# The opening of a two-layer decoder trunk: every block of tokens turned once, unscaled, and scaled behind the turn

## The chip, the cores and the metric

The kernel runs on one core of one Trainium2 chip. The metric is the device time of one execution in microseconds; the time given for a kernel is the median of its runs. In the profile TensorE is PE (its weight loads PEld), VectorE is DVE, ScalarE is ACT, GpSimd is POOL, and SP is the queue that issues nearly all DMAs.

## The reference

x is a stream of 1024 tokens of 1024 features in float32. There are two layers; each normalises x, makes all projections from it in one matrix, mixes tokens in two ways, and then runs a gated feed-forward part. Only the beginning of the first layer matters here:

```
def rmsnorm(x, g):
    xf = x.astype(jnp.float32)
    y = xf * lax.rsqrt(jnp.mean(xf * xf, axis=-1, keepdims=True) + RMS_EPS)
    return (y * g.astype(jnp.float32)).astype(x.dtype)
...
for l in range(DEPTH):
    h = rmsnorm(x, norm1[l])
    proj = h @ w_in[l]
    qa, ka, va, qb, kb, vb, gate_pre = jnp.split(proj, splits, axis=-1)
    ...
    x = x + merged @ w_o[l]
    h2 = rmsnorm(x, norm2[l])
    ...
return rmsnorm(x, norm_f)
```

## The kernel before, in words

**Numbers in two parts.** A float32 product is made from three TensorE passes: each operand is a rounded part `hi` and the rest `lo`, and `product` (lines 182 to 184) issues hi x hi, hi x lo and lo x hi. `split` (lines 141 and 148) makes the parts: ACT casts to `hi`, DVE subtracts to `lo`. For h the parts are `hh` and `hl`. TensorE wants features on the partitions, so h is held turned: `H[n]` holds the parts for token half n (512 tokens), with eight feature blocks `k` of 128. Beside it, `RAW[n, k]` holds the turned h unsplit (`h_raw`); its only readers are sums of blocks, made by DVE behind the last block's `hl`.

**The opening** is the generator `first()`. It brings in x in eight blocks of 128 tokens (`xr`, four buffers; the load of a block waits until the block four before it is released). For each block ACT squares and sums (line 2006) and takes the root (line 2007), DVE takes the reciprocal (line 2008): the factor of each token, in `factor[i]`. Then there are two forms.

- Blocks 0, 1 and 2: DVE multiplies the block in token order by the factor and the gain in two instructions of 128x512 (line 2015); the gain for that is spread over all partitions once, by eight transposes into the banks `gb` (line 2078). The scaled block `xsq` is turned by eight transposes (line 1997, `x_t`), and `in_two` splits it straight out of the bank. As the residual needs x turned and unscaled, `xr` is turned too, by eight more transposes, and copied by ACT to `x_part` (line 2024, `kept`); pairs of blocks are stored to DRAM as `xs` (line 2026).
- Blocks 3 to 7: the block is turned once, unscaled, and copied to `x_part`. One transpose spreads the factor over the partitions (line 2036, `x_rb`). DVE multiplies `x_part` by gain and factor, eight instructions of 128x128 (line 2040), into `RAW`; `split` makes the parts from there.

`RAW[0]` is missing blocks 0 to 2 that way; `again` (line 2055) lets GpSimd add `hh` and `hl` for these 384 tokens, in two groups of four additions, when blocks 4 and 5 are handled. A memset of `slots` on GpSimd is ordered behind them.

The weights of the first product (`w_raw`, four pairs of feature blocks) are cast by ACT (`weights_hi`) and their rest is subtracted by DVE for pairs 0 and 2, by GpSimd for pairs 4 and 6 (`weights_lo`, line 1990).

**What sets the order.** TensorE runs in the order of the text in the whole kernel. `mixer` alternates one step of `first()` with units of the first product (`v_ps`, twelve matmuls each, four feature blocks of one token block; later `kq_ps` and `q_ps`): setup and block 0, a unit; block 1's transposes, a unit; block 2's transposes, two units; block 3's, two units, and so on. A unit uses the block one or two behind the one just turned. ACT and DVE run in the order of the text up to block 2 (though a planner may slip other instructions in between); from block 3 on the planner orders them by readiness and priority, and `tc.high_priority` lifts an instruction. `fill(n)` is n matmuls of the identity whose result is not used; each is two passes in the profile.

## Time and profile before

| | |
|---|---|
| median of 3 runs | 2615.91 us (2615.09 to 2616.14) |
| profiled execution | 2618.04 us, its span 2616.1 us |
| TensorE busy in the span | 2606.0 us |
| DVE busy | 2089.5 us |
| ACT busy | 1357.6 us |
| GpSimd busy | 102.2 us |

A row of the timeline gives start and duration in us, the engine, the line, the operation, output<-inputs, shapes and count; in brackets stands the time that the engine had idled before it, and what ended that. Several instructions in a row are merged with their total. Starts count from the beginning of the span. The windows give for each stretch the busy time of each engine and its number of instructions.

### The profile page before, as it was taken

The numbers are of one execution on the slowest core, as the hardware profiler recorded it, in microseconds if no ns is written. First come the engines' busy times: TensorE is split into PE (matmuls) and PEld (weight loads), VectorE is DVE, ScalarE is ACT, GpSimd is POOL, SyncE is SP. The second block draws the span as 40 slices with busy tenths as digits, with TensorE's granted clock in tenths as the row PEclk, the third lists the DMA queues.
The fourth block names the chain that finished last, engine by engine and source line by source line (L and its number), as shares of the span: only waits on it lengthen the run. The fifth ranks groups of instructions, "written<-read, shape, count | busy, mean of one in ns | idle before, by whom it ended". The sixth has DMA issues, their size and how long they took to land.

```text
span 2616.1 us, 36210 instructions
## 1 busy us (share of the span) xinstructions
PE 2606.0 (100%) x12736; PEld 2185.2 (84%) x12736; DVE 2089.5 (80%) x3484; ACT 1357.6 (52%) x2533; POOL 102.2 (4%) x135
## 2 busy tenths in 40 slices
PE   9999999999999999999999999999999999999999
PEld 8888888888888888888888888888888888888888
DVE  7877777795988888897677788777869888889965
ACT  6555666574554555422445555666645555544225
POOL 3000000020000000000000000000300000000000
PEclk9999999999999999999999999999999999999999
DMA  7434578873344444688344436787633344447962
GB/s 254 151 120 132 161 207 217 214 247 93 93 145 153 145 164 142 234 326 317 145 145 147 125 128 180 203 231 210 207 99 119 125 161 146 150 164 260 347 238 111
DMA packets 400418, 468.22 MB, mean 179 GB/s; under 512 B 24308, under 2 KB 315500, under 8 KB 398444
## 3 DMA queue, kind: packets, MB, share of 16 engines
q1 hardware_dynamic: 400220, 465.90, 55.3%
q8 instruction: 101, 1.65, 0.3%
q14 instruction: 81, 0.66, 0.1%
q10 hardware_dynamic: 16, 0.00, 0.0%
HBM read 303.23 MB, written 162.59 MB: 178 GB/s over the span
## 4 chain that ended last, share of the span: by engine, by line
PE 96%; DVE 1%; DMA 1%; ACT 1%; issue 1%; SPq 0%; POOL 0%; DVEq 0%; ACTq 0%
PE u_a L1019 6%; PE u_a L1018 6%; PE u_a L1017 6%; PE d_ps L1780 5%; PE d_ps L1781 5%; PE d_ps L1782 5%; PE i_a L1017 5%; PE i_a L1019 5%; PE i_a L1018 5%; PE u_c L1017 3%; PE u_c L1019 3%; PE u_c L1018 3%; PE i_c L1017 3%; PE i_c L1019 3%; PE i_c L1018 3%; PE o_ps L183 2%
## 5 line engine op out<-in xcount | busy, mean ns | idle before, releaser
L141 ACT CAST w_hi<-up_a 128x512 fp32r<-128x512 f32 x280 | 173.9, 622 | 276.5 <-DVE up_a L1634 120.5
L148 DVE TENSOR_TENSOR w_lo<-up_a,w_hi 128x512 fp32r<-128x512 f32 x280 | 189.3, 688 | 83.6 <-ACT w_hi L141 83.6
L141 ACT CAST w_hi<-in_a 128x512 fp32r<-128x512 f32 x252 | 156.2, 622 | 162.9 <-PE i_c L1018 38.0
L148 DVE TENSOR_TENSOR w_lo<-in_a,w_hi 128x512 fp32r<-128x512 f32 x252 | 172.7, 687 | 75.8 <-ACT w_hi L141 67.0
L1788 DVE TENSOR_TENSOR x<-x,d_ps 128x512 f32<-128x512 f32 (+1 forms) x228 | 153.4, 674 | 65.0 <-PE d_ps L1782 61.6
L1780 PE MATMUL d_ps<-gd_in,w_hi 128*128 128x512 f32 (+1 forms) x340 | 130.0, 382 | 0.0
L1782 PE MATMUL d_ps<-gd_in,w_lo 128*128 128x512 f32 (+1 forms) x340 | 129.8, 382 | 0.0
L1781 PE MATMUL d_ps<-gd_in,w_hi 128*128 128x512 f32 (+1 forms) x340 | 129.7, 382 | 0.0
L1019 PE MATMUL u_a<-hh,w_lo 128*128 128x512 f32 x320 | 124.5, 389 | 0.0
L1018 PE MATMUL u_a<-hl,w_hi 128*128 128x512 f32 x320 | 124.5, 389 | 0.0
L1017 PE MATMUL u_a<-hh,w_hi 128*128 128x512 f32 x320 | 124.5, 389 | 0.0
L1017 PE MATMUL u_a<-t_hi,w_hi 128*128 128x512 f32 x320 | 124.5, 389 | 0.0
L1019 PE MATMUL u_a<-t_hi,w_lo 128*128 128x512 f32 x320 | 124.5, 389 | 0.0
L1018 PE MATMUL u_a<-t_lo,w_hi 128*128 128x512 f32 x320 | 124.5, 389 | 0.0
L1017 PE MATMUL i_a<-hh,w_hi 128*128 128x512 f32 x288 | 119.2, 414 | 0.0
L1017 PE MATMUL i_a<-t_hi,w_hi 128*128 128x512 f32 x288 | 118.3, 411 | 0.0
L1780 PE MATMUL d_ps<-gd_in,wd 128*128 128x512 f32 (+1 forms) x292 | 113.9, 390 | 0.0
L1019 PE MATMUL i_a<-hh,w_lo 128*128 128x512 f32 x288 | 113.2, 393 | 0.0
L1019 PE MATMUL i_a<-t_hi,w_lo 128*128 128x512 f32 x288 | 113.0, 393 | 0.0
L1018 PE MATMUL i_a<-t_lo,w_hi 128*128 128x512 f32 x288 | 112.9, 392 | 0.0
L1018 PE MATMUL i_a<-hl,w_hi 128*128 128x512 f32 x288 | 112.8, 392 | 0.0
L1782 PE MATMUL d_ps<-gd_in,wd 128*128 128x512 f32 (+1 forms) x292 | 112.8, 386 | 0.0
(380 smaller groups left out, 7834.9 us busy)
## 6 DMA issues: line engine op xcount, KB each, us to landing
gd<-g SPq DMA_DIRECT2D x154, 512.0 KB, 3.3
gd_in<-gd SPq DMA_DIRECT2D x154, 512.0 KB, 5.9
up_a<-in_w_up_dram SPq DMA_DIRECT2D x80, 512.0 KB, 5.2
in_a<-in_w_in_dram SPq DMA_DIRECT2D x72, 512.0 KB, 5.3
wd_raw<-in_w_down_dram SPq DMA_DIRECT2D x22, 1024.0 KB, 11.2
gin<-gs SPq DMA_DIRECT2D x32, 512.0 KB, 3.8
w_raw<-in_w_o_dram SPq DMA_DIRECT2D x64, 256.0 KB, 2.9
gs<-u SPq DMA_DIRECT2D x48, 256.0 KB, 3.2
```

What stands on the lines that cost most here:

```text
L141: one = act.copy(hi, src)
L148: two = dve.tensor_tensor(lo, src, f32(hi), ALU.subtract)
L183: pe.matmul(o, lh, rl, start=False, stop=False, skip_group_check=share)
L1017: pe.matmul(o, w[0][:, c], rh, start=(first and i == 0), stop=False, skip_group_check=True)
L1018: pe.matmul(o, w[0][:, c], rl, start=False, stop=False, skip_group_check=True)
L1019: pe.matmul(o, w[1][:, c], rh, start=False, stop=(last and i == 3), skip_group_check=True)
L1780: pe.matmul(o[:, sub], wh[:, c], gh[:, sub], start=(i == 0 and k in (0, 4, 5)), stop=False, skip_group_check=True)
L1781: pe.matmul(o[:, sub], wh[:, c], gl[:, sub], start=False, stop=False, skip_group_check=True)
L1782: pe.matmul(o[:, sub], wl[:, c], gh[:, sub], start=False, stop=(i == m - 1), skip_group_check=True)
L1788: dve.tensor_tensor(x, x, o[:, sub], ALU.add)
```

## The change

Blocks 0, 1 and 2 get the form of the others: turned once, unscaled, copied to `x_part`, multiplied there into `RAW[0]`, split from there. The token-order multiplication, its spread gain `gb` and `again` are gone, and with them the second set of transposes for three blocks. `normed` is cut into `spread` (the transpose of the factor), `normed` (the eight multiplications) and `halved` (cast and subtraction of one half). In block 0 the second group of four fills stands behind the spread, and GpSimd subtracts for weight pair 0, DVE for pairs 2, 4 and 6. The memset of `slots` is ordered behind the last weight subtraction of GpSimd.

```diff
--- before.py
+++ after.py
@@ -671,7 +671,7 @@
             R["kv"] = sb.tile([P, 2, T], F32R, tag="xa", bufs=4, name="kv")
             R["slots"] = sb.tile([P, 4, 2, 256], F32R, tag="xa", bufs=4, name="slots")
             one = pool.memset(f32(R["slots"][64:128, :, 1, :]), 0.0)
-            tc.add_manual_dep(one.ins, LAST["again"], NO_SYNC, reason="behind")
+            tc.add_manual_dep(one.ins, LAST["pools"][3], NO_SYNC, reason="behind")
         t = slice(256 * qp, 256 * qp + 256)
         k, q = (y[u // 2][:, u % 2, :, t] for y in (sk, sq))
         for x in range(2):
@@ -1963,10 +1963,9 @@
     def first():
         g_raw = sb.tile([KD, P], F32, tag="ot", name="g_raw")
         nc.scalar.dma_start(g_raw, norm1[0].rearrange("(c p) -> c p", p=P))
-        gb = [bank("o", "gb") for _ in range(2)]
         warm = sb.tile([P, 8], F32, tag="ss", bufs=2, name="warm")
         act.activation(warm[:, 0:1], eps, AF.Sqrt)
-        xr, rest, tps, parts, factor, raw_t, part = {}, {}, {}, {}, {}, {}, {}
+        xr, parts, factor, raw_t, part = {}, {}, {}, {}, {}
         raw = big("w_raw").rearrange("p a (b c) -> p (a b) c", c=256)
         wv = early["wv"] = []
 
@@ -1998,9 +1997,7 @@
             return [tp.rearrange("p (e t) -> p e t", e=4) for tp in got]
 
         def scaled(i):
-            if i in (0, 2):
-                rest["pair"] = big("xsq")
-            sq = rest[i] = rest["pair"][:, i % 2, :] if i < 4 else sb.tile([P, T], F32, tag="ot", name="xsq")
+            sq = sb.tile([P, T], F32, tag="ot", name="xsq")
             ss = factor[i] = sb.tile([P, 8], F32, tag="ss", bufs=2, name="ss")
             with tc.high_priority(offset=AHEAD):
                 act.activation(sq, xr[i], AF.Square, accum_out=ss[:, 0:1])
@@ -2008,12 +2005,6 @@
                 one = dve.reciprocal(ss[:, 2:3], ss[:, 1:2])
             if i == 0:
                 tc.add_manual_dep(one.ins, LAST["base"], NO_SYNC, reason="in turn")
-            yield
-            if i not in (3, 4, 5, 6, 7):
-                for h in range(2):
-                    hd = slice(h * HF, (h + 1) * HF)
-                    dve.scalar_tensor_tensor(sq[:, hd], xr[i][:, hd], ss[:, 2:3], gb[h], ALU.mult, ALU.mult)
-            yield
 
         def kept(i):
 
@@ -2025,36 +2016,24 @@
             if i % 2:
                 nc.sync.dma_start(xs[i // 4][:, :, (i % 4 - 1) * P : (i % 4 + 1) * P], part["pair"].rearrange("p k i t -> p k (i t)"))
 
-        def normed(i):
+        def spread(i):
+
+            rb = bank("o", "x_rb")
+            pe.transpose(rb[:, 0:P], factor[i][:, 2:3].to_broadcast([P, P]), ident)
+            return rb
+
+        def normed(i, rb):
 
             n, c = i // 4, i % 4
             if c == 0:
                 new_h(n)
-            if i in (3, 4):
                 raw_h(n)
-            rb = bank("o", "x_rb")
-            pe.transpose(rb[:, 0:P], factor[i][:, 2:3].to_broadcast([P, P]), ident)
-            for h in range(2):
-                hf = RAW[n, h][:, :, c * P : (c + 1) * P]
-                for k in range(4 * h, 4 * h + 4):
-                    dve.scalar_tensor_tensor(hf[:, k - 4 * h, :], part[i][:, k, :], g0[:, k : k + 1], rb[:, 0:P], ALU.mult, ALU.mult)
-                LAST["h"] = split(*(y[:, 4 * h : 4 * h + 4, c * P : (c + 1) * P] for y in H[n]), hf).ins.name
-
-        def in_two(i, *halves):
-            n, c = i // 4, i % 4
-            if c == 0 and 1 not in halves:
-                new_h(n)
-            for h in halves or range(2):
-                split(*(y[:, 4 * h : 4 * h + 4, c * P : (c + 1) * P] for y in H[n]), tps[i][h])
-
-        def again(k):
-
-            t = slice(0, 3 * P)
-            for e in range(4 * k, 4 * k + 4):
-                hi, lo = (f32(y[:, e, t]) for y in H[0])
-                one = pool.tensor_tensor(RAW[0, k][:, e - 4 * k, t], hi, lo, ALU.add)
-                tc.add_manual_dep(one.ins, LAST["pools"][1 + 2 * k], NO_SYNC, reason="behind")
-            LAST["again"] = one.ins.name
+            for k in range(KD):
+                dve.scalar_tensor_tensor(RAW[n, k // 4][:, k % 4, c * P : (c + 1) * P], part[i][:, k, :], g0[:, k : k + 1], rb[:, 0:P], ALU.mult, ALU.mult)
+
+        def halved(i, h):
+            n, t = i // 4, slice(i % 4 * P, (i % 4 + 1) * P)
+            LAST["h"] = split(*(y[:, 4 * h : 4 * h + 4, t] for y in H[n]), RAW[n, h][:, :, t]).ins.name
 
         def fill(n):
 
@@ -2074,55 +2053,36 @@
         pe.transpose(wp[:, 0:KD], g_raw, ident[0:KD, 0:KD])
         LAST["g0"] = dve.tensor_copy(g0, wp[:, 0:KD]).ins.name
         masks()
-        for k in range(KD):
-            pe.transpose(gb[k // 4][:, (k % 4) * P : (k % 4 + 1) * P], g0[:, k : k + 1].to_broadcast([P, P]), ident)
-        f = [scaled(i) for i in range(8)]
-        next(f[0])
+        fill(4)
+        scaled(0)
         weights_hi(0)
+        raw_t[0] = turned(xr[0], "t")
+        kept(0)
+        rb = spread(0)
+        fill(4)
+        weights_lo(0, pool)
+        normed(0, rb)
+        halved(0, 0)
         weights_hi(2)
-        fill(4)
-        next(f[0])
-        tps[0] = turned(rest[0], "s")
-        fill(1)
-        weights_lo(0)
-        in_two(0, 0)
         weights_lo(2)
-        in_two(0, 1)
-        next(f[1])
+        halved(0, 1)
+        scaled(1)
         weights_hi(4)
         weights_hi(6)
-        next(f[1])
-        weights_lo(4, pool)
-        weights_lo(6, pool)
+        weights_lo(4)
+        weights_lo(6)
         yield
         for i in range(1, 8):
             load(i + 2)
-            if i in (3, 4, 5, 6, 7):
-                for j in {1: (0,), 2: (1,), 3: (2,)}.get(i, ()):
-                    raw_t[j] = turned(xr[j], "t")
-                    kept(j)
-                raw_t[i] = turned(xr[i], "ts"[i % 2])
-                with tc.high_priority(offset=AHEAD) if i == 3 else nullcontext():
-                    kept(i)
-                    normed(i)
-                if i in (4, 5):
-                    again(i - 4)
-                if i < 7:
-                    for _ in f[i + 1]:
-                        pass
-            else:
-                for j in {1: (0,), 2: (1,), 3: (2,)}.get(i, ()):
-                    raw_t[j] = turned(xr[j], "t")
-                    if j not in (0,):
-                        kept(j)
-                tps[i] = turned(rest[i], "s")
-                if i < 7:
-                    for _ in f[i + 1]:
-                        pass
-                in_two(i)
-                for j in {1: (0,), 2: (1,), 3: (2,)}.get(i, ()):
-                    if j in (0,):
-                        kept(j)
+            raw_t[i] = turned(xr[i], "ts"[i % 2])
+            with tc.high_priority(offset=AHEAD) if i == 3 else nullcontext():
+                kept(i)
+                normed(i, spread(i))
+            if i < 7:
+                scaled(i + 1)
+            with tc.high_priority(offset=AHEAD) if i == 3 else nullcontext():
+                halved(i, 0)
+                halved(i, 1)
             yield
 
     def setup(l):
```

## The prediction

> **What bounds the kernel now.** I read the page first, then the busy time by stretches of the opening, then the opening in order of time, engine by engine. The page:
>
> ```profile
> span 2616.1 us, 36210 instructions
> PE 2606.0 (100%) x12736; PEld 2185.2 (84%) x12736; DVE 2089.5 (80%) x3484; ACT 1357.6 (52%) x2533; POOL 102.2 (4%) x135
> ...
> PE 96%; DVE 1%; DMA 1%; ACT 1%; issue 1%; SPq 0%; POOL 0%; DVEq 0%; ACTq 0%
> ```
>
> TensorE is busy for 2606.0 of 2616.1 us and is 96% of the chain. So only three things move the end: TensorE work taken away or added, the start of its dense run, and waits that open inside it. The stretches that the change touches (columns: stretch, length, busy time and count of PE, PEld, DVE, ACT, POOL, clock, DMA):
>
> ```profile
> 0.00:10.00 10.00, 7.75 (x35) 7.04 (x35) 4.38 (x12) 5.10 (x10) 2.83 (x15) 1.00 0.76 258
> 10.00:20.00 10.00, 9.65 (x78) 8.87 (x78) 6.01 (x13) 9.52 (x21) 6.26 (x6) 1.00 0.72 234
> 20.00:30.00 10.00, 10.00 (x88) 9.92 (x87) 8.22 (x24) 9.09 (x20) 3.93 (x4) 1.00 0.99 303
> 30.00:40.00 10.00, 10.00 (x55) 8.46 (x54) 9.32 (x22) 5.80 (x13) 9.44 (x9) 1.00 0.96 309
> ```
>
> TensorE idles 2.25 us in the first ten and 0.35 us in the next ten, and not at all after 20 us. All that can be won by better waits is therefore under 2.6 us; the rest must come from work that TensorE no longer does. DVE has 4 us free between 10 and 20 us, and ACT only 0.5 us: the cover for new vector work is there, but behind a full ACT.
>
> **The change on TensorE.** The timeline of TensorE from the first fill to the first transpose of block 4:
>
> ```profile
> 3.91 1.97 PE L2078 MATMUL gb<-ident,g 128*128 128x128 f32 x8 [0.26 <-DVE g L2075]
> 5.67 1.91 PE L2062 MATMUL warm<-ident 128*128 128x128 f32 x8
> 7.38 1.71 PE L1997 MATMUL x_t<-ident,xsq 128*128 128x128 f32 x8
> 8.92 0.39 PE L2062 MATMUL warm<-ident 128*128 128x128 f32 x2
> 9.50 0.39 PE L182 MATMUL v_ps<-w_hi,hh 128*128 128x256 f32 x1 [0.19 <-ACT hh L141]
> 10.23 0.39 PE L184 MATMUL v_ps<-w_hi,hl 128*128 128x256 f32 x1 [0.22 <-DVE hl L148]
> 11.54 1.04 PE L1997 MATMUL x_t<-ident,xr 128*128 128x128 f32 x8
> 12.44 1.23 PE L1997 MATMUL x_t<-ident,xsq 128*128 128x128 f32 x8
> 14.49 0.19 PEld L183 LDWEIGHTS v_ps<-w_lo,hh 128*128 128x128 f32 x1 [0.21 <-POOL w_lo L1990]
> 15.47 0.91 PEld L1997 LDWEIGHTS x_t<-ident,xr 128*128 128x128 f32 x8 [0.33 <-ACT x_part L2024]
> 16.45 1.07 PE L1997 MATMUL x_t<-ident,xsq 128*128 128x128 f32 x8
> 17.28 0.36 PE L182 MATMUL v_ps<-w_hi,hh 128*128 128x256 f32 x1
> 20.23 1.97 PE L1997 MATMUL x_t<-ident,xr 128*128 128x128 f32 x16
> 22.03 0.27 PE L2036 MATMUL x_rb<-ident,ss 128*128 128x128 f32 x1
> 25.01 1.04 PE L1997 MATMUL x_t<-ident,xr 128*128 128x128 f32 x8
> ```
>
> Between 11.54 and 25.01 stand six sets of eight transposes: the raw blocks 0, 1, 2, 3 and the scaled blocks 1, 2. After the change three are left there (raw 1, 2, 3; raw block 0 takes the place of scaled block 0 in front of them). A set costs 0.9 us (11.54 to 12.44; two sets from 20.23 to 22.03 in 1.80). Removed: 3 x 0.9 = 2.7 us. Added: two transposes that spread the factor (blocks 1 and 2), 0.11 us each at the pitch of a set, 0.2 us; that of block 0 lies in the wait for its own data. The eight gain transposes into gb at 3.91 go, but they lie under the arrival of x and count nothing. The two idle times in this stretch (0.21 and 0.33 us) can go too. So 2.5 us of work and up to 0.5 us of waits: at most 3.0 us to win.
>
> **The change on ACT and DVE.** Here every block gets what only blocks 3 to 7 had: two copies out of the bank, eight small multiplications, two casts, two subtractions. The rows that price them, and the rows of block 3, which has this form already:
>
> ```profile
> 4.63 1.06 ACT L2006 ACTIVATE xsq<-xr 128x1024 f32<-128x1024 f32 x1 [1.71 <-DMA xr<-in_x_dram]
> 6.02 0.60 ACT L1984 CAST w_hi<-w_raw 128x512 fp32r<-128x512 f32 x1
> 6.14 0.16 DVE L2008 RECIPROCAL ss<-ss 128x1 f32<-128x1 f32 x1 [0.69 <-ACT ss L2007]
> 6.41 1.41 DVE L2015 SCALAR_TENSOR_TENSOR xsq<-xr,ss,gb 128x512 f32<-128x512 f32 x2
> 8.87 1.06 ACT L141 CAST hh<-x_t 128x512 fp32r<-128x512 f32 x2
> 11.90 2.54 POOL L1990 TENSOR_TENSOR w_lo<-w_raw,w_hi 128x512 fp32r<-128x512 f32 x2 [8.44 <-ACT w_hi L1984]
> 14.82 1.08 ACT L2024 COPY x_part<-x_t 128x512 f32<-128x512 f32 x2
> 18.19 1.05 ACT L2006 ACTIVATE xsq<-xr 128x1024 f32<-128x1024 f32 x1
> 22.63 1.90 DVE L2040 SCALAR_TENSOR_TENSOR h_raw<-x_part,g,x_rb 128x128 f32<-128x128 f32 x7 [0.55 <-ACT x_part L2024]
> 24.67 0.77 DVE L148 TENSOR_TENSOR hl<-h_raw,hh 128x512 fp32r<-128x512 f32 x1
> 26.38 0.69 DVE L148 TENSOR_TENSOR hl<-h_raw,hh 128x512 fp32r<-128x512 f32 x1 [0.61 <-ACT hh L141]
> 34.67 4.82 POOL L2055 TENSOR_TENSOR h_raw<-hh,hl 128x384 f32<-128x384 f32 x4
> 42.79 0.28 PE L182 MATMUL v_ps<-w_hi,hh 128*128 128x256 f32 x1
> 45.32 0.69 DVE L148 TENSOR_TENSOR hl<-h_raw,hh 128x512 fp32r<-128x512 f32 x1 [0.69 <-ACT hh L141]
> ```
>
> Pitches: a small multiplication 0.26 us (1.90 for seven, overlapped), so a block 2.1 us; a cast or copy of half a block 0.53 us; a subtraction 0.6 to 0.7 us; Square, its read-out and the root 1.39 us on ACT (4.63 to 6.02). Over the opening DVE gets 24 x 0.26 = 6.2 us and one w_lo more (0.6), and loses 6 x 0.70 = 4.2 us: 2.6 us net. ACT's total doesn't change. On both engines the order of blocks 0 to 2 is the order of the text, so it can be followed by hand:
>
> *Block 0.* The four fills (eight passes) now start at 3.91, in the place of gb, and take 1.7 us; raw x_t(0) follows at 5.6 (x is there at 4.6) and is out at about 7.3, its factor spread by 7.5. DVE multiplies from 7.5: half 0 is ready at 8.6, half 1 at 9.7. The cast of half 0 ends at 9.3, so the first v_ps comes at 9.4 instead of 9.50; but its subtraction stands behind all eight multiplications, 9.7 to 10.3, so the third v_ps comes at 10.4 instead of 10.23. First twelve matmuls: 0.1 to 0.2 us later. w_lo(0) now runs on GpSimd (2.54 for two, so 1.3 us) from 6.6 to 7.9, hidden until 9.4. If the second group of fills must wait until the copies have emptied the banks of x_t(0), at 7.9, it ends near 9.5: another 0.1 us at most.
>
> *Block 0, second half.* Cast, w_hi(2), cast, then Square(1) at 10.35: ACT reaches w_hi(4) at 11.75 and w_hi(6) at 12.3. DVE does w_lo(4) 12.4 to 13.0 and w_lo(6) to 13.6. TensorE has x_t(1) from 11.65 and the spread by 12.65, waits 0.4 us for w_lo(4), and ends this half at 14.45; before, it did so at 15.1 (15.47 - 0.33). The wait on GpSimd's w_lo is gone, DVE's is late next.
>
> *Block 1.* This is the tight place. DVE can multiply only behind w_lo(6): 13.6 to 15.7. The factor of block 2 is behind it (15.85), and TensorE has the spread of block 2 queued in front of the matmuls of block 1; it was free at 15.45. hl of block 1's half 0 ends at 16.5. So TensorE stands from 15.45 to 16.05 and again to 16.55: 1.0 us. The 24 matmuls (17.28 to 20.23, so 2.95 us) end at 19.2, before at 20.23.
>
> *Blocks 2 and 3.* x_t(3) and the spread: 1.0 us, to 20.2. DVE multiplies block 2 from 17.1 to 19.1; its half 0 of hl is there at 20.0, in time, if the cast isn't held up. In the row at 18.19 Square(4) runs before the casts of block 2, put there by its priority; the same order now puts 1.2 us more of ACT ahead of them, and hl comes at 21.2: TensorE waits 0.75 us. Block 4's transposes start at 23.1 without it and at 23.85 with it, 25.01 before. The gain is 1.9 or 1.15 us; with no reason to choose I take **1.5 us**.
>
> *After that* nothing should take it back. Block 4 is first used at 42.79 and block 7 three blocks (3 x 2.95 us) later, at 51.6; its hl ended at 46.0 before. DVE's 2.6 us more would fit into that distance of 5.6 us even if none of it fell into the 4 us that DVE had free before 20 us. Beyond that cover the cost is what exceeds 5.6 us.
>
> *The rest, at nothing.* GpSimd's adds of h (4.82 for the second four) go from an engine whose sums are read only behind block 7's hl; the memset tied to them only moves forward. The loads of blocks 4 to 7 are queued on SP behind the release of the x buffers, and those are released when a raw block is turned: earlier now by what the second turning took. That can only help or cost nothing, unless ACT meets a Square whose x has not landed (a rival, below). The stores of pairs move ahead on SP too, into a stretch where DMA is busy for 0.72 of the time, not 0.99.
>
> **Time.** The profiled execution has a span of 2616.1 us and took 2618.04 us, 1.9 us around it and 2.1 us above the median of 2615.91. The change lies inside the span, so I subtract from the median: 2615.91 - 1.5 = **2614.4 us**. About 0.2% (5.2 us) is what a measurement of this kernel can tell from no change, and no sum here comes near it.
>
> **Rivals.**
> - *No wait opens.* If block 1's chain is a little shorter than I follow it, TensorE keeps 3.0 us less the 0.2 of the first matmuls: 2613.1 us. For it: in block 3 the multiplications began 0.6 us after the spread and TensorE never waited. Against: block 1 has w_lo(4) and w_lo(6) ahead of it on DVE.
> - *The chain per block takes the place of the transposes* (slower than before). From the spread of block 3 (22.03) to its first hl passed 3.4 us, to its second 5.0 us (26.38 + 0.69). TensorE has 3.9 us of other work (2.95 + 1.0) between the turning of blocks 2 and 3 and their first use, and less for block 1. If a Square is put ahead of the casts in each of them (1.4 us, longer where x hasn't landed), the waits are 1.0 + 1.4 for block 1 and 3.4 + 1.4 - 3.9 = 0.9 each for blocks 2 and 3, 4.2 us: 4.2 - 3.0 + 0.2, so 1.4 us slower, 2617.3 us. It decides where the first hl comes over 3.9 us behind the spread. For it: ACT is busy for 9.52 of 10 us there. Against: the ACT order of these blocks is written out, and only the Squares of later blocks can slip in.
> - *TensorE gets up to its fast pace later.* A set of transposes took 1.71 us at 7.38 and 1.04 us at 11.54: the pace doubled near 8.8 us, behind fills and transposes without a gap from 3.91. The new order has a gap of some 0.6 us between the spread and the second fills. If the fast pace came one set of transposes and two groups of twelve matmuls later, the price is 0.7 + 2 x 1.4 = 3.5 us, of which 1.1 us falls into the wait before block 1: 2.4 us, 2614.4 + 2.4 = 2616.8 us. For it: no row shows how long a gap the pace bears. Against: the gap is small, and there are three fills more. [...]
> - *Another order far behind the opening.* ACT, DVE, GpSimd and SP are ordered by a planner that sees the shifted opening. If that opens waits of several us in later stages, the result leaves the 0.2% band; the page shows no stage where TensorE is short of work, so this is rare.
>
> **How the numbers follow.** Forecast 47%; no wait 18%; chain per block 18%; late pace 9%; another order 8%, of which 2 beyond the band on the fast side, 4 on the slow side, 2 within. So faster by over 0.2%: 0.02, within: 0.94, slower: 0.04. The range reaches from the full gain with its idle time and 1 us of difference between runs (2612.1) to the slow chain with the same allowance (2618.3).
>
> **What would show it.** In the new profile: 64 transposes of xr and none of xsq; no gain transposes; 64 small multiplications instead of 40; no add of h on GpSimd. Right: the first v_ps near 9.4, its first L184 near 10.4, a wait of about 1 us before the third matmul of block 1 near 16.5 with DVE's hl as releaser, block 4's transposes between 23.1 and 23.9, and from there the same distances as before, shifted as a whole. Wrong: transposes at the slow pace after 9 us; a TensorE wait over 1.5 us before blocks 2 or 3; block 4's transposes at 25 or later; or a shift that grows or shrinks behind 60 us.

## The result and the profile after

| | before | after |
|---|---|---|
| median of seven runs each, us | 2615.40 (2615.01 to 2616.14) | 2623.24 (2621.69 to 2625.34) |
| profiled execution, us (span) | 2618.04 (2616.1) | 2621.69 (2619.8) |

The changed kernel takes 1.0030 of the time before, 95% interval 1.0019 to 1.0041: 7.8 us more. The forecast was 2614.4 us, in a range that ended at 2618.3. So the change made the kernel slower, by a little more than what can be told from no change.

The head of the page after, with the shares of the chain that ended last:

```profile
span 2619.8 us, 36166 instructions
...
PE 2603.9 (99%) x12713; PEld 2182.9 (83%) x12713; DVE 2089.6 (80%) x3503; ACT 1358.7 (52%) x2533; POOL 93.8 (4%) x126
...
PE 97%; DVE 1%; ACT 1%; DMA 1%; issue 0%; SPq 0%; DVEq 0%; ACTq 0%
```

TensorE is busy for 2.1 us less (2606.0 to 2603.9), and the span is 3.7 us longer. What was gained in work was lost in idle time. The busy time by stretches of 10 us of the changed kernel says where (columns as in the prediction):

```profile
0.00:10.00 10.00, 5.92 (x32) 5.15 (x32) 3.63 (x15) 5.13 (x10) 4.10 (x16) 1.00 0.78 266
10.00:20.00 10.00, 8.12 (x59) 7.08 (x60) 9.39 (x25) 9.49 (x20) 4.57 (x6) 1.00 0.65 207
20.00:30.00 10.00, 7.41 (x51) 7.00 (x50) 6.37 (x20) 6.06 (x14) 3.37 (x3) 0.83 1.01 354
30.00:40.00 10.00, 10.00 (x68) 9.06 (x67) 8.93 (x29) 8.26 (x18) 0.00 (x0) 1.00 0.42 150
```

TensorE is idle for 8.55 us of the first 30 (2.60 before), and between 20 and 30 us its granted clock is 0.83 instead of 1.00. TensorE's timeline in that stretch, the rows that answer to those of the prediction:

```profile
5.72 0.60 PE L1996 MATMUL x_t<-ident,xr 128*128 128x128 f32 x4
7.34 0.66 PE L1996 MATMUL x_t<-ident,xr 128*128 128x128 f32 x4 [1.02 <-ACT x_part L2015]
10.05 0.38 PE L182 MATMUL v_ps<-w_hi,hh 128*128 128x256 f32 x1 [1.05 <-ACT hh L141]
11.04 0.39 PE L184 MATMUL v_ps<-w_hi,hl 128*128 128x256 f32 x1 [0.48 <-DVE hl L148]
16.86 0.32 PE L2022 MATMUL x_rb<-ident,ss 128*128 128x128 f32 x1 [0.41 <-DVE ss L2005]
18.22 0.39 PE L184 MATMUL v_ps<-w_hi,hl 128*128 128x256 f32 x1 [0.80 <-DVE hl L148]
20.95 1.04 PE L1996 MATMUL x_t<-ident,xr 128*128 128x128 f32 x8
25.67 0.39 PE L182 MATMUL v_ps<-w_hi,hh 128*128 128x256 f32 x1 [2.15 <-ACT hh L141]
26.61 0.58 PE L184 MATMUL v_ps<-w_hi,hl 128*128 128x256 f32 x1 [0.44 <-DVE hl L148]
26.99 0.42 PE L182 MATMUL v_ps<-w_hi,hh 128*128 128x256 f32 x1
28.91 1.33 PE L1996 MATMUL x_t<-ident,xr 128*128 128x128 f32 x8
```

The row at 25.67 is the main one: 2.15 us of idle time before the second half of block 2 (the second of its two groups of twelve matmuls), where the prediction had no wait. Behind it a matmul lasts 0.42 us where it lasted 0.28. Block 4's transposes (28.91) come 3.9 us later than before (25.01), not 1.2 to 1.9 us earlier.

ScalarE shows why the cast came late:

```profile
20.68 0.61 ACT L141 CAST hh<-h_raw 128x512 fp32r<-128x512 f32 x1
21.59 0.59 ACT L2015 COPY x_part<-x_t 128x512 f32<-128x512 f32 x1 [0.30 <-PE x_t L1996]
...
22.27 0.58 ACT L2015 COPY x_part<-x_t 128x512 f32<-128x512 f32 x1
23.25 1.06 ACT L2003 ACTIVATE xsq<-xr 128x1024 f32<-128x1024 f32 x1 [0.41 <-DMA xr<-in_x_dram]
...
24.31 0.60 ACT L141 CAST hh<-h_raw 128x512 fp32r<-128x512 f32 x1
...
25.01 0.60 ACT L141 CAST hh<-h_raw 128x512 fp32r<-128x512 f32 x1
```

The cast at 20.68 is block 2's first half; it ends at 21.29. The second half's cast is the one at 25.01, though VectorE had finished its multiplications at 20.84 (18.69 + 2.15):

```profile
18.69 2.15 DVE L2032 SCALAR_TENSOR_TENSOR h_raw<-x_part,g,x_rb 128x128 f32<-128x128 f32 x8
```

Between them stand block 3's two copies, the Square of block 5, which waited for its x, and block 3's first cast (24.31). All of these carry a high priority; block 2's cast does not. And x of block 5 was late because of what SyncE's queue had ahead of it:

```profile
16.41 1.60 SPq L163 DMA_DIRECT2D w_raw<-in_w_in_dram  x2
18.11 0.45 SPq L1975 DMA_DIRECT2D xr<-in_x_dram  x1
18.65 0.64 SPq L2017 DMA_DIRECT2D xs<-x_part  x1
19.39 3.00 SPq L1975 DMA_DIRECT2D xr<-in_x_dram  x2
```

The second pair of loads of the first K and Q weights (16.41) has to wait until GpSimd is done with their buffers (the first of its subtractions there ends at 16.39); the load of block 5's x, at 18.11, stands in line behind it.

### The profile page after: what moved, and what is told of

Its sections match the earlier page's. It is cut to its first block, busy times and chain, and to the rows that moved or that the text cites. A ratio compares the mean times of both kernels' runs of the same rounds, so it can differ in the third digit from the quotient of the medians.

```text
span 2619.8 us, 36166 instructions
## 1 busy us (share of the span) xinstructions
PE 2603.9 (99%) x12713; PEld 2182.9 (83%) x12713; DVE 2089.6 (80%) x3503; ACT 1358.7 (52%) x2533; POOL 93.8 (4%) x126
## 4 chain that ended last, share of the span: by engine, by line
PE 97%; DVE 1%; ACT 1%; DMA 1%; issue 0%; SPq 0%; DVEq 0%; ACTq 0%
PE u_a L1018 6%; PE u_a L1017 6%; PE u_a L1019 6%; PE d_ps L1780 5%; PE d_ps L1782 5%; PE d_ps L1781 5%; PE i_a L1017 5%; PE i_a L1019 5%; PE i_a L1018 5%; PE u_c L1017 3%; PE u_c L1018 3%; PE u_c L1019 3%; PE i_c L1017 3%; PE i_c L1019 3%; PE i_c L1018 3%; PE o_ps L182 2%
```

## The experiments

**Theory A**: the loss is one of order. The planner, free to slip instructions between those of block 2, puts block 3's prioritised chain and the Square of block 5 ahead of block 2's second cast; TensorE waits, and its clock drops. **Theory B**: the loss is spread over the edits (block 0's bank, GpSimd beside VectorE, the x loads), or lies in later stages. **Theory C** came up on the way: in part of the executions TensorE gets to its quick pace late.

All runs in one table. "x_t(4)" and "x_t(7)" are the start of the transposes of blocks 4 and 7 in the profiled execution, "over before" is the median against that of the kernel before, measured beside it. The profiled execution is one of the run's own and lies up to 1.8 us off its median.

| run | x_t(4), us | x_t(7), us | span, us | median over before, us |
|---|---|---|---|---|
| before again (one execution) | 25.09 | 36.43 | 2614.8 | |
| after | 28.91 | 40.57 | 2619.8 | +7.8 |
| after again (one execution) | 29.58 | 41.31 | 2621.7 | |
| cast_first | 24.67 | 39.91 | 2619.6 | +6.3 |
| gap_filled | 28.75 | 40.10 | 2619.7 | +5.1 |
| first_bank | 30.53 | 42.21 | 2622.8 | +6.7 |
| x_loads_first | 29.54 | 42.36 | 2621.1 | +5.2 |
| squares_low | 27.30 | 38.64 | 2618.1 | +5.0 |
| order_only | 25.59 | 37.97 | 2618.6 | +2.8 |
| order_squares | 24.72 | 40.84 | 2620.4 | +3.9 |
| order_squares_loads | 23.77 | 35.76 | 2617.2 | +2.4 |
| all_four | 22.59 | 34.60 | 2615.2 | +2.3 |
| all_four_filled | 23.03 | 35.15 | 2614.3 | +0.7 |

**after_again**, the changed kernel itself:

> The changed kernel as it is, for a second profile. Theory A (a late cast and the TensorE clock): again a TensorE wait of about 2.2 us before the second twelve matmuls of block 2, near 23.5 us, ended by ACT's cast, and behind it a stretch of granted clock 0.5; how long that stretch lasts varies from run to run, and the time with it, 2621.7 to 2625.3 us. Theory B (something behind the opening that the planner ordered differently): the stretch and the wait may be there, but the difference to the kernel before goes on growing behind 30 us.

2623.61 us. The wait before block 2's second half is there again, 2.7 us long, and the clock drop too (0.50 from 27 to 30 us). So the late cast is not an accident of one execution. Against before again, the shift is 4.9 us at block 7's transposes and still 5.0 at the second layer's queries (1344 us); 1.2 us more come between 1874 and 1963 us.

**cast_first**: block 2's casts get block 3's priority.

```diff
-            with tc.high_priority(offset=AHEAD) if i == 3 else nullcontext():
+            with tc.high_priority(offset=AHEAD) if i in (2, 3) else nullcontext():
                 halved(i, 0)
```

> The change, and the cast and subtraction of block 2's halves get the priority that block 3's steps have, so that the planner puts block 2's second cast ahead of block 3's chain and of Square(5). Theory A: the 2.15 us wait and the half-clock stretch go, 4 us in the profile and more in the median, since the profile was of the fastest run: 2616 to 2618 us. What stays over the kernel before is the first block, 0.8 us later, and perhaps a new wait for block 3's second cast, which now stands behind Square(6). Theory B: no more than 1 us better than 2623.

2622.88 us (2619.89 to 2625.86), ratio 1.0023 (1.0014 to 1.0033). The place is confirmed and the remedy fails. Block 4's transposes come 4.2 us earlier than after, at 24.67, but then TensorE waits before block 3's second half. TensorE's row and ScalarE's (with priority, the Square of block 6 stands ahead of the cast of block 3, and its x lands late):

```profile
30.40 0.39 PE L182 MATMUL v_ps<-w_hi,hh 128*128 128x256 f32 x1 [2.26 <-ACT hh L141]
...
28.69 1.06 ACT L2003 ACTIVATE xsq<-xr 128x1024 f32<-128x1024 f32 x1 [1.63 <-DMA xr<-in_x_dram]
...
29.75 0.60 ACT L141 CAST hh<-h_raw 128x512 fp32r<-128x512 f32 x1
```

The wait moved on by one block. The 2616 to 2618 expected were missed; what the expectation had as a "perhaps", a new wait for block 3's second cast behind the Square of block 6, is what happened.

**gap_filled**: ten identity matmuls between the two groups of block 2, so that the wait stays and TensorE works through it.

```diff
-                for _ in range(2):
+                for u in range(2):
+                    if i == 0 and u == 1:
+                        keep = bank("o", "keep")
+                        for _ in range(10):
+                            pe.matmul(keep[:, 0:P], ident, ident, start=True, stop=True)
                     next(first_units, None)
```

> The change, with ten matmuls of the identity (twenty passes, 2.2 us at the fast pace) put between the two groups of twelve of block 2: the wait for the cast stays, TensorE only isn't idle in it. Theory A: the granted clock stays at 1.00 behind 26 us, block 4's transposes come near 27.3 instead of 28.9 us, the median falls by 1.5 us or more, to 2619.5 to 2622, and the runs lie closer together than 3.6 us. Theory B, and the theory that only the idle time counts: no change, 2623.

2621.66 us (2620.78 to 2622.83), ratio 1.0019 (1.0009 to 1.0029). The granted clock of the changed kernel in one stretch of the wait's aftermath, where its matmuls begin 0.21 us apart (26.99 to 28.70), and TensorE's rows of this run, where they begin 0.12 us apart (27.68 to 28.64):

```profile
27.00:28.00 1.00, 1.00 (x6) 0.50 0.97 351
```

```profile
23.60 2.39 PE L1327 MATMUL keep<-ident 128*128 128x128 f32 x20
26.51 0.39 PE L182 MATMUL v_ps<-w_hi,hh 128*128 128x256 f32 x1 [0.52 <-ACT hh L141]
27.45 0.39 PE L184 MATMUL v_ps<-w_hi,hl 128*128 128x256 f32 x1 [0.44 <-DVE hl L148]
28.75 1.04 PE L2000 MATMUL x_t<-ident,xr 128*128 128x128 f32 x8
```

From block 2's third matmul of the second half to block 4's transposes pass 1.30 us here (27.45 to 28.75), 2.30 after (26.61 to 28.91). So the half clock costs 1.0 us there and 0.3 in the transposes that follow (1.33 against 1.04 us); it is a consequence of the wait, not the loss itself. Block 4's transposes themselves came at 28.75, not near 27.3 as expected: in this execution the Square of block 5 waited 1.02 us for its x, and block 2's second cast came at 25.86, 0.85 us later than after.

In after the granted clock fell to 0.50 behind 2.15 us without a matmul, followed by two matmuls and another 0.44 us. A wait of 2.06 us (squares_low) and waits of 2.26 and 0.23 us with two matmuls between (cast_first) left the clock at 1.00; the last section sets these side by side.

**first_bank**: block 0 turned into the other pair of banks, since the warm-up holds one bank of "t" and block 0's two halves had to share the other.

```diff
-        raw_t[0] = turned(xr[0], "t")
+        raw_t[0] = turned(xr[0], "s")
...
-            raw_t[i] = turned(xr[i], "ts"[i % 2])
+            raw_t[i] = turned(xr[i], "st"[i % 2])
```

> The change, with block 0's transposes in the pair of banks that the warm-up fills don't use (the two pairs swapped for all blocks). The wait of 1.02 us between block 0's halves goes; first v_ps near 9.5 instead of 10.05 us. Theory A: the wait before block 2's second half ends when ACT's cast comes, and that stands behind Square(5) and the landing of x block 5 at 23.2 us, so the gain of 0.5 to 0.8 us is lost in a longer wait: the same 2622 to 2624 us. The rival (TensorE's total of waits is what counts): 0.5 to 1 us better.

2623.24 us (2621.86 to 2625.01), ratio 1.0025 (1.0016 to 1.0035). The wait of 1.02 us at 7.34 goes, and the wait before block 2's second half grows to 3.7 us, because the Square of block 5 waits 2.88 us for its x; the clock falls to 0.50 here too. A late resource further on takes the gain.

**x_loads_first**: the loads of the first K and Q weights go behind block 5's x on SyncE.

```diff
-            nc.sync.dma_start(raw, src[:, r : r + per, :])
+            one = nc.sync.dma_start(raw, src[:, r : r + per, :])
+            if eng:
+                tc.add_manual_dep(one.ins, LAST["load"], NO_SYNC, reason="behind")
```

> The change, and only the order of SP: the loads of the k and q weights (line 163) stand behind the loads of x blocks 4 and 5, where the changed kernel had the second pair of them, waiting 8 us for GpSimd to release their buffers, in front of block 5. ACT's order stays as it is. Theory A (ACT's cast of block 2 waits behind a Square whose x lands late): Square(5) no longer waits for a landing; the cast still stands behind block 3's first cast, so the wait before block 2's second half falls from 2.2 to about 1.5 us. GpSimd's work on these weights moves too: the two w_lo subtractions (1.71 us) and block 1's two hl (2.04 us) should be back at 1.3 us each pair, and the 0.8 us wait in block 1 at 0.3. Together 1 to 3 us better than 2623: 2620 to 2622. Rival (x was not late, only the order on ACT counts): 2623.

2621.36 us (2619.1 to 2622.93), ratio 1.0019 (1.001 to 1.0028). The time lies where it was expected, but the gain is given back. The Square of block 5 no longer waits for its x, and the wait for block 2's second cast falls to 1.23 us; the wait in block 1 falls from 0.80 to 0.22. Behind the cast there is a new wait of 1.37 us for block 2's second difference: GpSimd's work has moved to 24.5 us with the weights, and block 3's first difference, which stands ahead on VectorE, takes 1.53 us beside it instead of 0.69:

```profile
25.22 1.27 POOL L173 TENSOR_TENSOR kq_w<-w_raw,kq_w 128x512 fp32r<-128x512 f32 x1
25.51 1.53 DVE L148 TENSOR_TENSOR hl<-h_raw,hh 128x512 fp32r<-128x512 f32 x1
```

The clock falls to 0.50 behind these two waits as well. The run answers two other questions. First, GpSimd has nothing to do between 8 and 24 us, and VectorE's differences show what its company costs. Columns as in a timeline; from the changed kernel, then from this run:

```profile
12.96 1.71 DVE L1989 TENSOR_TENSOR w_lo<-w_raw,w_hi 128x512 fp32r<-128x512 f32 x2 [0.35 <-ACT w_hi L1983]
14.59 2.14 DVE L2032 SCALAR_TENSOR_TENSOR h_raw<-x_part,g,x_rb 128x128 f32<-128x128 f32 x8
...
16.73 2.04 DVE L148 TENSOR_TENSOR hl<-h_raw,hh 128x512 fp32r<-128x512 f32 x2
...
15.11 2.51 POOL L171 TENSOR_TENSOR kq_w<-w_raw,kq_w 128x512 fp32r<-128x512 f32 x2
```

```profile
13.70 1.29 DVE L1992 TENSOR_TENSOR w_lo<-w_raw,w_hi 128x512 fp32r<-128x512 f32 x2 [0.35 <-ACT w_hi L1986]
16.07 2.16 DVE L2035 SCALAR_TENSOR_TENSOR h_raw<-x_part,g,x_rb 128x128 f32<-128x128 f32 x8 [1.08 <-PE x_rb L2025]
...
18.39 1.29 DVE L148 TENSOR_TENSOR hl<-h_raw,hh 128x512 fp32r<-128x512 f32 x2
```

Two pairs of differences took 3.75 us beside GpSimd and 2.58 alone: 1.2 us on block 1's chain that the prediction did not have. Taken singly, only the difference that meets GpSimd's work is longer: of the pair at 16.73 the first took 1.44 us, begun 0.89 us before GpSimd's subtractions ended at 17.62, and the second, behind them, 0.68. The multiplications, which read the spread factor out of a bank, took the same in both. Before the change, block 1's pair of differences read x_t out of a bank and took 1.28 us beside the same GpSimd work:

```profile
15.53 1.28 DVE L148 TENSOR_TENSOR hl<-x_t,hh 128x512 fp32r<-128x512 f32 x2
```

So with both inputs in SBUF VectorE lost 0.75 us where the two engines met for 0.89 (1.44 against 0.69), and 0.84 us in the row at 25.51, where they met for 0.98 (1.53 against 0.69); the pair with one input in a bank took 1.28 us beside the same work. What lies behind this, the traces don't show.

Second, block 1 began at the half pace, two rows of TensorE in this run:

```profile
13.86 0.41 PE L186 MATMUL v_ps<-w_hi,hl 128*128 128x256 f32 x1
14.07 1.78 PE L1999 MATMUL x_t<-ident,xr 128*128 128x128 f32 x8
```

In this execution TensorE came to its quick pace near 15.6 us (its matmuls began 0.21 us apart up to 13.86 and 0.12 from 15.92), in order_only near 11.5, in the other profiles with the changed opening between 5.5 and 7.4. The windows give the granted clock as 1.00 in this stretch, though 0.21 us is the distance that the matmuls had in after at 0.50. That is where theory C is from.

**squares_low**: the Squares of blocks 4 to 7 lose their priority, and with them, under the same `with`, the roots and the reciprocals.

```diff
-            with tc.high_priority(offset=AHEAD):
+            with tc.high_priority(offset=AHEAD) if i < 4 else nullcontext():
                 act.activation(sq, xr[i], AF.Square, accum_out=ss[:, 0:1])
```

> The change, and the Squares from block 4 on lose their priority, so that the planner puts block 2's second cast and block 3's casts ahead of Square(5) and Square(6). SP's order stays. Theory A: the 2.15 us wait falls under 0.7 us, no stretch of half clock follows, and no cast that TensorE needs stands behind a landing: 2616 to 2619 us. Rival (the priority of block 3's chain is what delays the cast, the Squares don't matter): the wait stays near 2 us, 2621 to 2623.

2621.14 us (2619.62 to 2622.13), ratio 1.0019 (1.001 to 1.0028): the rival's time, not theory A's 2616 to 2619. The second cast now comes earlier, but the difference behind it waits on VectorE, which does block 3's prioritised multiplications and block 3's first difference ahead of it (22.20 to 25.26):

```profile
26.00 0.39 PE L184 MATMUL v_ps<-w_hi,hl 128*128 128x256 f32 x1 [2.06 <-DVE hl L148]
```

So no single instruction is to blame. Block 3's chain goes ahead of block 2's on both engines.

**all_four**: the order of ScalarE and VectorE written out through block 3 (the diff of order_only, below) with the three edits above (first bank, x loads, Squares).

> The change with four mends at once: ACT and DVE in the order of the text for block 3 too, Squares from block 4 on without priority, x loads ahead of the k and q weights, and block 0 in the banks that the fills don't use. Theory A: first v_ps near 9.5 us, no TensorE wait over 0.6 us behind 12 us and no half clock; block 7's transposes at 35 to 36.5 us (36.35 before, 40.6 with the change). The time is then that of the prediction's sum, 2613.5 to 2616.5 us, at or a little under the kernel before. Theory B (something behind the opening): still 3 us or more above the kernel before.

2618.41 us (2616.94 to 2620.02), ratio 1.0007 (0.9998 to 1.0016). TensorE's rows:

```profile
8.96 0.38 PE L184 MATMUL v_ps<-w_hi,hh 128*128 128x256 f32 x1 [1.05 <-ACT hh L141]
9.95 0.38 PE L186 MATMUL v_ps<-w_hi,hl 128*128 128x256 f32 x1 [0.48 <-DVE hl L148]
...
18.73 1.04 PE L1999 MATMUL x_t<-ident,xr 128*128 128x128 f32 x8
...
22.59 1.03 PE L1999 MATMUL x_t<-ident,xr 128*128 128x128 f32 x8
...
34.60 1.04 PE L1999 MATMUL x_t<-ident,xr 128*128 128x128 f32 x8
```

The opening that the prediction had summed exists: block 3's transposes at 18.73 (forecast 19.2), block 4's at 22.59 (23.1), block 7's 1.8 us earlier than before. It took four mendings of the change to get it, and the median does not show it: the 2613.5 to 2616.5 us expected were missed.

**before_again**, the kernel before itself:

> The kernel before as it is, for a second profile: the first profile was of an execution of 2618.04 us, 2.6 us above the median of the others, and in it TensorE had the slow pace until about 8.8 us, in both profiles of the change only until 5.7 to 7.9 us. If the pace explains the 2.6 us, this profile has it fast by 6 us, the first v_ps earlier than 9.5 us, and block 7's transposes 1 to 2.5 us earlier than 36.35 us.

2616.78 us. TensorE had its quick pace from 5.7 us, earlier than in the first profile (near 9), and block 7's transposes start at 36.43, no earlier. The expectation of 1 to 2.5 us was missed: before the change the pace of the first microseconds is hidden. The 1.3 us between the two profiles of before arise behind the opening: matmul against matmul, 0.7 near 590 us and 0.8 between 1880 and 1970, less 0.2 between.

**order_only**: of the four mendings only the order.

```diff
-                for n in (1, 2):
+                for n in (1, 2, 2):
                     next(pending)
                     for _ in range(n):
                         next(first_units)
...
-                if i == 3:
+                if i == 2:
                     dense.prime(1)
```

> Of the four mendings that went together into the version with all four, only the written order of ScalarE and VectorE is kept here: it reaches through block 3 (and the values' first weights are primed one block earlier), so block 3's prioritised copies and sums and the Squares of blocks 3 and 4 can no longer be placed ahead of block 2's second cast. Theory A (the loss is the planner's placing of block 3 ahead of block 2's cast): the waits of 2.15 and 0.44 us before block 2's second half go, TensorE's clock stays at 1.00 to 30 us, block 4's transposes come at 23.3 to 24.3 instead of 28.91, and the median is 2.5 to 4.5 us under the changed kernel's 2623.2: 2618.7 to 2620.7. The Square of block 5 can still stand ahead of block 3's cast with its x late, so a wait of up to 1.5 us may stay there. Rival (the loss is spread over bank, contention and loads and the order is a small part): x_t(4) at 26 or later and over 2621.5.

2619.4 us (2617.2 to 2620.91), ratio 1.001 (1.0001 to 1.0019). This is the run that speaks for A against B: 5.0 of the 7.8 us go with two lines that change no operation. (The intervals of the two ratios, 1.0019 to 1.0041 and this one, just meet.) TensorE waits before block 2 for 0.53 us, once, its clock stays at 1.00, and ScalarE does block 2's casts ahead of block 3's copies:

```profile
20.64 0.62 ACT L141 CAST hh<-h_raw 128x512 fp32r<-128x512 f32 x1 [0.51 <-DVE h_raw L2032]
21.67 0.62 ACT L141 CAST hh<-h_raw 128x512 fp32r<-128x512 f32 x1 [0.41 <-DVE h_raw L2032]
...
22.67 1.08 ACT L2015 COPY x_part<-x_t 128x512 f32<-128x512 f32 x2
```

Block 4's transposes came at 25.59, not at 23.3 to 24.3; 0.9 us of that lie in the late pace of this execution (block 1's transposes at 13.13, in order_squares at 12.21).

**order_squares**: the order, and the Squares without priority.

> The written order through block 3, and the Squares of blocks 4 to 7 without priority; first bank and load order as in the changed kernel. Theory A: no wait over 1 us before any half of a block from 1 on, block 4's transposes at 23.3 to 24.0, x_t(7) at 35.4 to 36.4 (before: 36.4), median 2618.0 to 2619.8; against the version with all four (2618.4) what is lacking is block 0's bank wait (0.5 to 0.8) and GpSimd beside block 1's differences (up to 1.1). Rival (x loads behind the second pair of weights are a cause of their own): a wait of 1 us or more for a copy or Square of block 4 or 5 stays, and 2620 or more.

2620.49 us (2618.73 to 2622.28), ratio 1.0015 (1.0006 to 1.0024): above order_only, where 2618.0 to 2619.8 had been expected. Up to block 6's transposes (32.81) it is ahead; then ScalarE waits for the x of block 6, the Square comes late, and TensorE waits for block 6's factor:

```profile
30.38 1.06 ACT L2003 ACTIVATE xsq<-xr 128x1024 f32<-128x1024 f32 x1 [2.42 <-DMA xr<-in_x_dram]
...
36.45 0.48 PE L2022 MATMUL x_rb<-ident,ss 128*128 128x128 f32 x1 [2.60 <-DVE ss L2005]
```

So the rival named in its expectation holds: the x loads are a cause, once the order is mended. They are not the whole of this wait. The Square is done at 31.4, but its root runs at 33.90, behind block 5's casts and copies, and its reciprocal at 36.23, behind block 5's eight multiplications, since both lost their priority with the Square. The clock falls to 0.50 behind the wait.

**order_squares_loads**: the same with the x loads first, which is all_four without the bank.

> As the run with order and Squares, and the loads of x blocks 2 to 5 ahead of the first kq weights; the first bank stays as in the changed kernel. So this is the version with all four but the bank. Theory A: block 0's second half of transposes waits 0.7 to 1.0 us again, everything after lies 0.5 to 0.8 us later than with all four: first v_ps near 9.6 to 10.0, x_t(4) at 23.1 to 23.5, median 2618.7 to 2619.5. If the bank is worth nothing (a later wait takes it up): 2618.0 to 2618.6.

2619.02 us (2617.63 to 2619.35), ratio 1.0008 (0.9999 to 1.0017). Behind the first fills no wait over 1.1 us is left. Block 4's transposes come at 23.77 (expected 23.1 to 23.5), 1.2 us behind all_four's; the medians differ by 0.1 us over before. The bank is worth a microsecond in the profile, and nothing that the medians tell.

**all_four_filled**: all_four with eight instead of four identity matmuls ahead of block 0's first product.

```diff
         rb = spread(0)
-        fill(4)
+        fill(8)
```

> The version with all four, with eight identity matmuls instead of four (16 passes, about 1.8 us at the quick pace) between block 0's spread and its first product, where TensorE stood idle 1.05 us. All four's profiled execution reached the quick pace at about 6 us and took 2617.24, its median is 2618.41; the execution of the run with x loads first that was profiled kept the half pace to 15.6 us at a granted clock of 1.00 and was 1.6 us over its median. Theory C (in part of the executions the quick pace comes late, because TensorE is idle before block 0's products, and that is what keeps all four above before): lowest time unchanged, spread under 2 us, median 2616.3 to 2617.5. Rival (the remaining 2.3 us lie elsewhere, in later stages): median 2618 to 2619.5, spread as before, 2.5 to 3.5 us. If the fills only delay the first product: first v_ps at 9.5 or later and 2619 or more.

2617.38 us (2616.3 to 2619.33), ratio 1.0004 (0.9995 to 1.0013). The median lies where theory C put it, the spread (3.0 us) does not, and the intervals of this run and of all_four overlap. In the profiled execution the first product waits for 0.16 us instead of 1.05. Theory C is neither shown nor refuted. This is the best version, and it can't be told from before: nothing here beats both kernels.

## Why the prediction was wrong

*TensorE's savings: right.* The 2.1 us less of busy time show little, since the two profiles of before differ by 1.6 us in it (2606.0, 2604.4). But with the order mended, block 4's transposes came 2.5 us earlier than before (25.09 to 22.59) in all_four, inside the "at most 3.0 us to win".

*Block 0: 0.6 us too early.* Forecast 9.4 and 10.4, measured 10.05 and 11.04. The copies and the transposes share one bank of "t" (row at 7.34). The prediction thought of the copies emptying the banks only for the fills behind them, at 0.1 us; the two halves of block 0 themselves had to take turns. With the other banks: 8.96 and 9.95.

*Block 1: the wait right, its price not.* Forecast two waits with 1.0 us; measured 0.41 and 0.80 for the factor and hl, the releasers as named. But block 3's transposes came at 20.95 instead of 19.2. Besides block 0's 0.6 us, the two pairs of differences were lengthened by GpSimd, by 1.2 us together; the prediction had taken the price of a difference from rows in which GpSimd was idle or nearly so.

*Blocks 2 and 3: the step that failed.* The prediction said that block 2's half 0 comes in time "if the cast isn't held up", and then allowed for one thing ahead of it, Square(4), 1.2 us. It did not follow the second half, nor ask what else carries a priority: block 3's copies, its multiplications and its first cast, and Square(5). Together they held block 2's second cast from 21.29, when ScalarE was done with the first, to 25.01, and TensorE for 2.15 + 0.44 us, and the half clock came on top with 1.0 us or more. Two of the prediction's own signs of being wrong were there: a TensorE wait over 1.5 us before block 2, and block 4's transposes behind 25 us. The rival "the chain per block takes the place of the transposes" is this mechanism, at its place and past its point of decision, but it was given 18% and a price of 0.9 us per block. Against it was held that the order of these blocks is written out; but an order that is written out for some instructions does not keep others from being slipped in between them, as the same sentence said of the Squares.

*"That can only help or cost nothing", said of the loads of x: wrong.* Block 4's was let go earlier (issued at 8.08, before at 12.64), but block 5's stood on SyncE behind weights that had to wait for GpSimd (rows at 16.41 to 19.39) and left at 18.11, before at 16.68. The exception the prediction made, a Square whose x has not landed, is what happened.

*"After that nothing should take it back": right for the changed kernel, not for the mended one.* From block 4's transposes on TensorE runs the same matmuls in the same order in all these kernels, so their starts can be compared one by one. The changed kernel is 3.8 us behind before again at block 4's transposes, 4.1 at block 7's, 4.1 at the first product of the values behind the first queries (47.01 against 42.87) and 4.5 at the last matmul. all_four loses in the same stretch: it is ahead by 2.5 us at block 4's transposes, by 1.8 at block 7's and by 1.35 at that product (41.52). Behind the opening every kernel, the one before included, picks up to 1.9 us against before again, in steps of 0.2 to 1.3 us that come in some executions and not in others, most of them near 590, 1565 and 1885 us. One wait of TensorE that goes with them stands near 589 us in before's first profile and near 1886 in after_again: 0.5 us for an `hl` that GpSimd makes (line 1399). No run shows a stage there that answers to the change.

*What stays open.* In the two profiles after, 4.1 to 4.9 us of the loss are seen in the opening, of 7.8 in the medians; the profile of after is of the fastest of its seven executions, 1.55 us under their median. And all_four has a median 2.3 us over before. In its profile the opening is not the reason, and neither is it in that of order_squares_loads, which reaches the first product of the values behind the queries at 42.87, as before again does, and has a median 2.4 us over before. From there to the last matmul all_four gives back 1.2 us, most of it in steps of 0.45 near 146 us and 0.8 near 1883, and order_squares_loads 1.9 in four such steps. Behind the last matmul pass 5.45 us in both profiles of before and 5.99 in ten of the twelve others, these two among them, because the last store of the output lands 0.6 us later (3.1 us from its issue in after, 2.5 in before). Why, whether the change brings these steps on, and whether executions that were not profiled lose by them or by the late pace, the runs don't tell.

## What to carry to other kernels

When a change removes the reason for an order, follow the planner as well as the durations: list for each engine which instructions carry a priority and could be put ahead of the one that TensorE waits for, and for each of them whose data it waits for itself. A mending that lifted or lowered one instruction moved such a wait to the next block (cast_first) or to the other engine (squares_low); what helped was to write out the order as far as the new chain reaches. Price an operation by a row with the same places of its inputs and the same neighbours at work.

## What the hardware did that was not expected

- In the opening the granted clock fell to 0.50 in five profiles: after, after_again, first_bank, x_loads_first and order_squares. In after it fell at 26.10 us and was back at 1.00 at 29.52, 3.41 us later; the windows of 2 us give 3.4 us for each of the other four (0.95, 0.50 and 0.70 from 26 to 32 us in first_bank).
- How long TensorE was busy ahead of a fall doesn't tell the waits apart by itself. In the 3.41 us before it, it was busy for 1.26 us in after; by estimates from the windows and waits for 0.5 in after_again and first_bank, 1.05 in order_squares and 1.6 in x_loads_first. In cast_first the clock stayed at 1.00, and of the 3.41 us from 28.14 on TensorE was busy for 0.92 (30.40 to 30.90 and 31.13 to 31.55).
- The times at which the trace has the clock change in after, 5.62 (its first record), 26.10, 29.52 and 2616.82 us, lie 6, 1 and 758 times 3.413 us apart; in before 8.74 (the first) and 2613.11 lie 763 times as much apart. The author's estimate from these times is that it depends on where a wait falls between them whether it costs the clock; it was not shown, since the clock of cast_first and squares_low changes nowhere in the stretch of their waits. With the gap filled (gap_filled) the matmuls behind it began 0.12 us apart, in after 0.21.
- At the start TensorE runs at about half its later pace, up to a time that differs from execution to execution: a set of transposes took 1.78 us at 14.07 in x_loads_first, 1.04 at 12.34 in after and 1.03 at 13.13 in order_only. In after and in before the pace changes where the trace's first record of the clock stands, at 5.62 and 8.74 us. The windows print 1.00 ahead of that record and behind it, while in before a set took 1.71 us ahead of it (7.38) and 1.04 behind it (11.54).
- A difference of two SBUF operands on VectorE took 0.68 us alone. In the two rows where it began beside a subtraction of GpSimd it took longer by nearly the time that the two met: 1.44 us with 0.89 us in common (after), 1.53 with 0.98 (x_loads_first). With one operand from a bank, a pair took 1.28 us beside the same work (before), as long as a pair of two SBUF operands alone (1.29, x_loads_first).
